# A quarter of w_o by a seven-product block scheme, woven with the rest of w_o by the list scheduler

## The chip, the cores and the metric

The kernel runs on one core of one Trainium2 chip. The metric is the device time of one execution in microseconds. The kernel before took 1211.24 us (median of three runs, 1210.77 to 1211.61); one more execution was taken with the profiler.

## The reference

One layer of a hybrid decoder trunk with 16 meta tokens and 256 tokens of width 2048, all in float32. The part that the change touches is the output projection of the mixer, `m @ W_o`, between the two gated branches and the first residual:

```python
u = rms_norm(h, g_pre_mix[l])
proj = u @ w_in[l]
...
m = jax.nn.sigmoid(gate_a) * y_a + jax.nn.sigmoid(gate_b) * y_b
h = h + rms_norm(m @ w_o[l], g_post_mix[l])
u = rms_norm(h, g_pre_mlp[l])
f = jnp.square(jax.nn.relu(u @ w_up[l])) @ w_down[l]
h = h + rms_norm(f, g_post_mlp[l])
```

`w_o` is 2048 x 2048, `w_up` 2048 x 8192, `w_down` 8192 x 2048. Only the 256 tokens go on after the mixer; they are two tiles of 128.

## The kernel before

**Arithmetic.** Every float32 product is made of three TensorE products: a value is split into a high part (float32r, a copy on ACT) and a low part (the difference, a subtraction on DVE), and high x high, high x low and low x high are summed in PSUM. So each weight chunk of 1 MB (four 128-row blocks by 512 columns) passes through ACT (`high`, line 253) and DVE (`low`, line 256) before TensorE can use it, and the activations are kept in both parts.

**Streaming.** `stream` (from line 188) lists all chunks up to the first columns of w_up. `open_chunk` (line 233) takes the next: it starts the load into one of three `raw` buffers on SP's queue, and appends the two splits. `fetch` (line 273) opens and splits two chunks ahead and hands out the oldest. The split parts lie in three buffers each (`part_tile`, line 226, number modulo 3). `spare` (line 204) gives up-chunks 1 and 2 rooms of their own in the tags s0 and s1.

**The mixer's end.** The conv-out projection (`project_t` with `evac_conv`, lines 814 to 830) makes the mixed features m in token order, 512 columns at a time; `to_features` (line 803) turns them with four TensorE transposes for each token tile and splits them into `m`.

**w_o.** Four column blocks `n` of 512, each four chunks `kc` deep. For the first three, `project_t` (line 693) runs, for each chunk, 12 matmuls for token tile 0 and 12 for tile 1 (`block_t`, line 683: the 128 x 128 block of m is stationary, 512 columns of the weight chunk stream past it). `evac_o` (line 884) takes the sum of squares (ACT) and multiplies by g (DVE). The last column block goes by `project_t_but_two` and `project_t_two` (lines 706 and 715): its last two chunks are run for tile 0 first and for tile 1 afterwards, so that tile 0's norm, residual and turn (lines 941 to 998) run under tile 1's products. Lines 931 to 935 open three up-chunks there and split them; the low part of the third follows at line 999.

**After it.** w_up and w_down are planned by `Plan` (line 22): each piece of work is added with its engine, a cost in us and the names that it reads and writes; `order` gives each a due time, which follows from TensorE's fixed order, and lists the pieces engine by engine as they could begin. w_down already goes by seven block products (steps P1 to P7 at line 1049) with sums of weight blocks on DVE (line 1120).

Lines that the prediction names: 688 (matmuls of `block_t`), 808, 810 and 811 (turn, copy, subtraction of m), 817 and 818 (evacuation of conv-out), 893 (residual), 910 (turn of h), 1132 and 1137 (splits inside the plan), 1286 (matmuls of w_down), 1308 (bank added to a block).

Of the kernel before, what the change touches and what calls it, by code (L numbers as in the profile page):

```python
# [100 lines left out]
def hybrid_block(ctx: ExitStack, tc: tile.TileContext, ins: dict, out: bass.AP):  # L101
# [39 lines left out]
    def misc_tile(name):  # L141
        return psB.tile([P, CW], F32, tag="misc", name=name)
# [66 lines left out]
    stream += columns(w_up, 0, KD, CW, HALF)  # L209
    FIRST = KD // HALF[0]  # L210
    opened = []
    at = {"n": 0}


    LINE = 16
    PLACES = {n: (2, 1) for n in standing_chunks}
    KEYS = [f"{tag}{b}" for tag in ("lo", "hi") for b in range(3)]
    ready = {}

# [3 lines left out]
    for key in KEYS:  # L223
        ready[key] = part_room(key, f"{key[:2]}_{key[2]}")

    def part_tile(tag, n):
        key = f"{tag}{n % 3}"
        room = ready.pop(key) if key in ready else part_room(key, f"{tag}_{n}")
        place = PLACES.get(n, (1, 1))[("hi", "lo").index(tag)]
        shift = (place - 1 - 3 * KEYS.index(key)) % 4 * LINE  # L230
        return room[:, shift:shift + CK * CW]

    def open_chunk(first=((2, nc.sync),) * 4):
        n = at["n"]
        at["n"] += 1
        src, (rows, width) = stream[n]
        raw = raws.tile([P, CK * CW], F32, tag="raw", name=f"raw_{n}")
        if n in spare:
            both = big.tile([P, 2, CK * CW], F32R, tag=spare[n], name=f"parts_{n}")
            hi, lo = both[:, 0, :], both[:, 1, :]  # L240
        else:
            hi, lo = part_tile("hi", n), part_tile("lo", n)
        raw, hi, lo = (t.rearrange("p (k c) -> p k c", k=rows) for t in (raw, hi, lo))
        pieces = rows if n < FIRST + 1 else 1
        k = rows // pieces
        i = 0
        for n_, queue in first if n < FIRST else ((rows, nc.sync),):
            sl = slice(i, i + n_)
            queue.dma_start(raw[:, sl, :], src[:, sl, :])
            i += n_  # L250

        def high(sl):
            nc.scalar.copy(hi[:, sl, :], raw[:, sl, :])  # L253

        def low(sl):
            nc.vector.tensor_sub(lo[:, sl, :], raw[:, sl, :], f32(hi[:, sl, :]))  # L256
# [7 lines left out]
        todo = [piece(i) for i in range(pieces)]  # L264
        if n in spare:
            todo = [lambda: high(slice(0, rows)), lambda: low(slice(0, rows))]
        opened.append((hi, lo, todo))

    def split_pieces(c):
        while opened[c][2]:  # L270
# [2 lines left out]
    def fetch(ahead=2):  # L273

        for c in range(ahead + 1):
            if c == len(opened) and at["n"] < len(stream):
                open_chunk()
            if c < len(opened):
                split_pieces(c)
        flush()  # L280
        return opened.pop(0)[:2]
# [421 lines left out]
            while after:  # L703
                after.pop(0)()

    def project_t_but_two(act, nk, accs):

        n = nk // CK
        for kc in range(n - 2):
            hi, lo = fetch()  # L710
            for t, acc in enumerate(accs):
                block_t(acc, hi, lo, act, kc, nk, t)
        return [fetch(1), fetch(0)]

    def project_t_two(act, nk, accs, two, t):

        for i, (hi, lo) in enumerate(two):
            block_t(accs[t], hi, lo, act, nk // CK - 2 + i, nk, t)


    sg = [None, None]

# [80 lines left out]
    def to_features(n, t, mt):  # L803

        def f():
            pt = misc_tile(f"mt_{n}_{t}").rearrange("p (k c) -> p k c", k=CK)
            for i in range(CK):
                nc.tensor.transpose(pt[:, i, :], mt[:, i * P:(i + 1) * P], ident)
            dst = m[:, n * CK:(n + 1) * CK, :, t * P:(t + 1) * P]
            nc.scalar.copy(dst[:, :, 0, :], pt)  # L810
            nc.vector.tensor_sub(dst[:, :, 1, :], pt, f32(dst[:, :, 0, :]))
        return f

    def evac_conv(n):
        def f(t, acc):
            mt = mts[:, (n * NT + t) % (CC // CW * 2), :]
            nc.vector.tensor_mul(mt, acc, sg[1][:, t, block(n)])
            nc.vector.tensor_add(mt, mt, sg[0][:, t, block(n)])
            blocks.append(to_features(n, t, mt))
        return f  # L820

    def s_act_of(k):
        return ln["out"][:, k, :, :]

    mts = big.tile([P, CC // CW * 2, CW], F32, tag="c", name="mts")
# [5 lines left out]
    after += blocks  # L831


    h1 = big.tile([P, NT, D], F32, tag="k8", bufs=2, name="h1")
    nc.gpsimd.dma_start(h1, xv)
    g_mix = big.tile([P, D], F32, tag="a", name="g_mix")
    nc.gpsimd.dma_start(g_mix, ins["g_post_mix"].broadcast_to([P, D]))
    og = big.tile([P, NT, D], F32, tag="k8", bufs=2, name="og")

    class Norm:  # L840

# [37 lines left out]
        nc.scalar.activation(junk, src, AF.Square, scale=scale, accum_out=norm[:, t, n:n + 1])  # L879

    def last_factor(dst, acc, n):
        nc.vector.tensor_mul(dst, acc, g_mix[:, block(n)])

    def evac_o(n):
        def f(t, acc):
            square_of(acc, norm1.ssq, t, n)
            last_factor(og[:, t, block(n)], acc, n)
            if n == NB - 2:
                norm1.start(t)
        return f  # L890

    def residual(t, n):
        nc.vector.scalar_tensor_tensor(
# [44 lines left out]
    def last_block(t):  # L938
        last_factor(og[:, t, block(NB - 1)], last_o[t], NB - 1)
# [10 lines left out]
        for i in range(CK):  # L950
            low(i)

    block_t(last_o[1], *two[0], m_of, NB - 2, KD, 1)
    block_t(last_o[1], *two[1], m_of, NB - 1, KD, 1, (0, 1))
    both(u2_tiles(0, 1, 0, CK))
    block_t(last_o[1], *two[1], m_of, NB - 1, KD, 1, (2, 3))
    square_of(last_o[1], norm1.ssq, 1, NB - 1)
    high, low = u2_tiles(0, 1, CK, CK)
    chain = norm1.steps(1)
# [8 lines left out]
    residual(1, 0)  # L968

    accs = acc_tiles("up00")  # L970
    ups = list(opened)
    opened.clear()

    def up_high(kc, t):

# [20 lines left out]
    last_block(1)  # L996
    residual(1, 3)
    residual(0, 3)
    ups[2][2].pop(0)()
    up_high(0, 1)  # L1000
    up_low(0)
    both(u2_tiles(1, 1, 2 * CK, CK))
# [101 lines left out]
            load(to_load.pop(0))  # L1104

    split_at = {}
    first_n = at["n"] - len(opened)
    for m_, (hi_, lo_, _) in enumerate(opened):
        split_at[m_] = {"hi": hi_, "lo": lo_}

    def weights(m_):

        while uses and uses[0][0] <= m_:
            done = len(last_use_order) - len(uses)
            _, what, raws_ = uses.pop(0)
            rooms = [room_at[r] for r in raws_]
            names = [f"raw{r}" for r in rooms]
            if what == "sum":
                a_, b_ = (room_of[r][:, :CK * CW] for r in rooms)
                plan.add("DVE", 2.29, lambda: nc.vector.tensor_add(a_, a_, b_),  # L1120
                         reads=names, writes=names[:1])
            else:
                box = split_at[m_] = {}
                raw = room_of[rooms[0]][:, :CK * CW]
                n, q = first_n + m_, (first_n + m_) % 3
                if products[m_][0][0] == "U":
                    PLACES[n] = (2, 1)
                rows, width = HALF if products[m_][0][0] == "U" else (CK, CW)

                def high():  # L1130
                    box["flat"] = part_tile("hi", n)
                    nc.scalar.copy(box["flat"], raw)  # L1132
                    box["hi"] = box["flat"].rearrange("p (k c) -> p k c", k=rows)

                def low():
                    lo = part_tile("lo", n)
                    nc.vector.tensor_sub(lo, raw, f32(box["flat"]))  # L1137
# [384 lines left out]
```

## Time and profile before

| | us |
|---|---|
| median of three runs | 1211.24 |
| profiled execution, its own time | 1211.07 |
| span of that execution, first to last instruction | 1209.1 |
| TensorE busy in the span | 1198.0 |
| VectorE (DVE) busy | 955.1 |
| ScalarE (ACT) busy | 615.9 |

The profile is of one execution on the core. PE rows are TensorE's matmuls, PEld its weight loads, POOL is GpSimd, and SPq and POOLq are the queues from which DMAs are issued. A row of a group gives the source line, the engine, the operation, output and input tiles, shape and count, then busy time, mean ns of one, and the idle time ahead of it with what ended it. A row of the timeline gives start, length, engine, line and operation; square brackets hold the idle time before it and its releaser. The conv-out projection runs from about 380 to 427 us, w_o from 427 to 515, and w_up and w_down from 515 on.

### The profile page before, as it was taken

What the parts mean: (1) busy time and instruction counts of PE and PEld (TensorE: products, weight loads), DVE (VectorE), ACT (ScalarE), POOL (GpSimd) and SP (SyncE); (2) the same over time, 40 slices, a digit from 0 to 9 for tenths busy, and PEclk for the clock granted to TensorE, in tenths of its full rate; (3) what the DMA queues carried; (4) which work ended last, traced back from release to release, by engine and by line L of the source; (5) the groups of instructions that cost most, each with busy time, mean ns of one, the idle gap of its engine ahead of it and who ended that gap; (6) DMA issues with size and microseconds to landing.
All of it is one profiled execution on the core that took longest, in us unless ns stands there. A gap on an engine that the chain in (4) does not pass through costs nothing.

```text
span 1209.1 us, 15692 instructions
## 1 busy us (share of the span) xinstructions
PE 1198.0 (99%) x6456; PEld 1040.1 (86%) x6456; DVE 955.1 (79%) x1039; ACT 615.9 (51%) x636; POOL 5.6 (0%) x17
## 2 busy tenths in 40 slices
PE   9999999999999999999999999999999999999996
PEld 9999988888888888898888888888888888888886
DVE  6799978999676654578988878878788778888756
ACT  7533344343584444465555564564554555555542
POOL 1000000000000000000000000000000000000000
PEclk9999999999999999999999999999999999999999
DMA  9655565556558655646475574674765764755841
GB/s 288 209 175 176 181 201 180 204 183 200 180 168 292 222 182 185 215 163 220 151 250 174 180 233 158 197 247 142 245 200 156 261 199 150 243 174 182 271 139 69
DMA packets 161510, 237.22 MB, mean 196 GB/s; under 512 B 4017, under 2 KB 91505, under 8 KB 160912
## 3 DMA queue, kind: packets, MB, share of 16 engines
q1 hardware_dynamic: 159648, 231.03, 58.4%
q0 software_dynamic: 624, 3.30, 0.7%
q10 hardware_dynamic: 1168, 1.91, 0.4%
q8 instruction: 50, 0.82, 0.3%
q14 instruction: 20, 0.16, 0.0%
HBM read 234.12 MB, written 2.10 MB: 195 GB/s over the span
## 4 chain that ended last, share of the span: by engine, by line
PE 99%; DVE 0%; DMA 0%; DVEq 0%; ACT 0%; issue 0%; ACTq 0%
PE bank_u L433 18%; PE acc_gate L688 14%; PE acc_up L1286 14%; PE bank_u L439 9%; PE bank_a L1286 7%; PE bank_b L1286 5%; PE acc_o L688 5%; PE acc_v L428 4%; PE acc_z L428 4%; PE acc_g L428 4%; PE acc_co L688 4%; PE acc_po L688 4%; PE acc_o_last L688 2%; PE acc_up L433 1%; PE bank_u L1286 1%; PE acc_up L439 1%
## 5 line engine op out<-in xcount | busy, mean ns | idle before, releaser
L433 PE MATMUL bank_u<-m,hi 128*128 128x512 f32 x960 | 329.9, 390 | 0.0
L253 ACT CAST hi<-raw 128x2048 fp32r<-128x2048 f32 (+1 forms) x114 | 180.5, 1596 | 226.5 <-PE acc_gate L688 71.5
L256 DVE TENSOR_TENSOR lo<-raw,hi 128x2048 fp32r<-128x2048 f32 (+1 forms) x114 | 215.0, 1895 | 74.6 <-ACT hi L253 74.2
L439 PE MATMUL bank_u<-m,lo 128*128 128x256 f32 x960 | 265.5, 277 | 0.0
L1137 DVE TENSOR_TENSOR lo<-raw_m,hi 128x2048 fp32r<-128x2048 f32 x85 | 194.4, 2289 | 58.3 <-ACT hi L1132 58.2
L1132 ACT CAST hi<-raw_m 128x2048 fp32r<-128x2048 f32 x85 | 162.5, 1912 | 137.9 <-PE bank_u L433 76.7
L433 PEld LDWEIGHTS bank_u<-m,hi 128*128 128x128 f32 x960 | 180.2, 188 | 37.9
L439 PEld LDWEIGHTS bank_u<-m,lo 128*128 128x128 f32 x960 | 180.3, 188 | 1.6
L688 PE MATMUL acc_gate<-hi,u 128*128 128x512 f32 x512 | 158.6, 390 | 0.0
L1286 PE MATMUL acc_up<-hi,forms 128*128 128x512 f32 x496 | 157.5, 389 | 0.0
L494 DVE SCALAR_TENSOR_TENSOR c<-a,taps,c 128x256 f32<-128x256 f32 x240 | 115.5, 484 | 7.1 <-ACT c L488 0.5
L688 PEld LDWEIGHTS acc_gate<-hi,u 128*128 128x128 f32 x512 | 96.1, 188 | 19.9
L1286 PEld LDWEIGHTS acc_up<-hi,forms 128*128 128x128 f32 x496 | 93.1, 188 | 19.5
L688 PE MATMUL acc_gate<-lo,u 128*128 128x512 f32 x256 | 99.6, 389 | 0.0
L1286 PE MATMUL acc_up<-lo,forms 128*128 128x512 f32 x248 | 96.6, 389 | 0.0
L1137 DVE TENSOR_TENSOR lo<-raw_c,hi 128x2048 fp32r<-128x2048 f32 x29 | 66.4, 2290 | 20.7 <-ACT hi L1132 20.7
L1286 PE MATMUL bank_a<-hi,forms 128*128 128x512 f32 (+1 forms) x256 | 82.0, 383 | 0.0
L1132 ACT CAST hi<-raw_c 128x2048 fp32r<-128x2048 f32 x29 | 55.3, 1908 | 50.7 <-PE bank_u L433 25.7
L1137 DVE TENSOR_TENSOR lo<-raw_a,hi 128x2048 fp32r<-128x2048 f32 x29 | 66.4, 2289 | 18.0 <-ACT hi L1132 18.0
L1132 ACT CAST hi<-raw_a 128x2048 fp32r<-128x2048 f32 x29 | 55.4, 1912 | 42.6 <-PE bank_u L433 19.4
L1286 PE MATMUL bank_b<-hi,forms 128*128 128x512 f32 (+1 forms) x200 | 63.7, 382 | 0.0
L688 PE MATMUL acc_o<-hi,m 128*128 128x512 f32 x192 | 59.6, 390 | 0.0
(275 smaller groups left out, 1766.4 us busy)
## 6 DMA issues: line engine op xcount, KB each, us to landing
raw<-in_w_in_dram SPq DMA_DIRECT2D x54, 1024.0 KB, 5.1
raw_m<-in_w_down_dram SPq DMA_DIRECT2D x37, 1024.0 KB, 5.4
raw_m<-in_w_up_dram SPq DMA_DIRECT2D x33, 1024.0 KB, 6.0
raw<-in_w_o_dram SPq DMA_DIRECT2D x16, 1024.0 KB, 5.2
raw_c<-in_w_down_dram SPq DMA_DIRECT2D x14, 1024.0 KB, 5.1
raw_a<-in_w_up_dram SPq DMA_DIRECT2D x13, 1024.0 KB, 5.8
raw_a<-in_w_down_dram SPq DMA_DIRECT2D x13, 1024.0 KB, 5.4
raw_c<-in_w_up_dram SPq DMA_DIRECT2D x12, 1024.0 KB, 5.7
```

What stands on the lines that cost most here:

```text
L253: nc.scalar.copy(hi[:, sl, :], raw[:, sl, :])
L256: nc.vector.tensor_sub(lo[:, sl, :], raw[:, sl, :], f32(hi[:, sl, :]))
L428: nc.tensor.matmul(acc, w[:, k[0], cs], act[:, k[1], a, off:], start=first and n == 0, stop=last and n == 2)
L433: nc.tensor.matmul(acc.rearrange("p (a t) -> p a t", a=2)[:, :, ts], hi[:, k[0], cs], act[:, k[1], :, off + ts.start:off + ts.stop], start ...
L439: nc.tensor.matmul(acc[:, :T], lo[:, k[0], cs], act[:, k[1], 0, off:], start=False, stop=stop, skip_group_check=True)
L494: nc.vector.scalar_tensor_tensor(c, conv["a"][:, q, i:i + T], taps[:, q, i:i + 1], c, op0=ALU.mult, op1=ALU.add)
L688: nc.tensor.matmul(acc, act(kk)[:, a_, ts_], w_[:, k, :], start=kk == 0 and n == 0, stop=kk == nk - 1 and n == 2)
L1132: nc.scalar.copy(box["flat"], raw)
L1137: nc.vector.tensor_sub(lo, raw, f32(box["flat"]))
L1286: nc.tensor.matmul(acc, forms[h][:, f, k, a_, :], box[w_][:, k, cs], start=start and k == 0 and n == 0, stop=stop and k == KH - 1 and n == ...
```

## The change

Write w_o's first two row blocks and first two column blocks as B11, B12, B21, B22 (each 512 x 512, the row block first) and m's tiles as A11, A12, A21, A22 (token tile first, then the 512-feature block). Instead of eight products A x B for this quarter, seven are formed, with sums of A's and of B's blocks (Winograd's form). `sums_of_m` forms the sums of A on DVE in place, from unsplit copies that `feature_steps` leaves in the tile `A`; `forms_o` splits them into `Sf`. The sums of B are formed in the raw rooms: B11 + B12 and B22 + B12 by a DMA from POOL's queue that adds what it loads to what lies there (`add_second`), the other two by DVE (`add_rooms`).

STEPS gives TensorE's order: `P1` to `P7` are the seven products (12 matmuls each), `Xnk` is column block n, row block k for both token tiles (24 matmuls), the last two of them for tile 0 alone. P2, P3 and P4 go straight into the banks of the result (`c00`, `c01`, `c10`); P1, P6, P7 sum up in bank `a` and P5 in `b`, from where ACT copies them to SBUF and DVE adds them to the result's banks. The raw chunks lie in five rooms: the three raw buffers and two in the tag s1 (free after the conv-out evacuation). The whole of w_o, the last turn of m, the evacuations of column blocks 0 to 2 and the loads and splits of the first three up-chunks are put into a `Plan` of their own. `stream` ends its w_o part after two chunks (row blocks 1 and 2 of column block 0), which are P2's and X02's.

```diff
@@ the stream
-    for n in range(NB):
-        stream += columns(w_o, 0, KD, n * CW)
-
-    spare = {len(stream) + 1: "s0", len(stream) + 2: "s1"}
+
+    stream += columns(w_o, CK, CK, 0) + columns(w_o, 2 * CK, CK, 0)
...
@@ the turn of m
+        def low():
+            nc.vector.tensor_sub(dst[:, :, 1, :], box["pt"], f32(dst[:, :, 0, :]))
+            if n < 2:
+                nc.scalar.copy(A[:, t, n], box["pt"])
...
+    def sums_of_m():
+
+        a11, a12, a21, a22 = (A[:, t, h] for t in range(2) for h in range(2))
+        nc.vector.tensor_sub(a11, a11, a21)
+        nc.vector.tensor_sub(a21, a21, a22)
+        nc.vector.scalar_tensor_tensor(a22, a11, -1.0, a22, op0=ALU.mult, op1=ALU.subtract)
+        nc.vector.tensor_add(a12, a12, a22)
...
@@ conv-out
-        after += blocks
+        after += blocks + [sums_of_m] * (n == 2)
...
@@ w_o
-    for n in range(NB - 1):
-        project_t(m_of, KD, evac_o(n), f"o{n}")
+    plan = Plan()
+    HALVES = ("hi", "lo")
+    SA1, SA2, SA3, SA4 = ((1, 0), (1, 1), (0, 0), (0, 1))
+    B_OF = {"P1": (0, 0), "P2": (1, 0), "P3": (1, 1), "P5": (0, 0), "P6": (0, 0), "P4": (0, 0),
+            "P7": (1, 1)}
+    A_OF = {"P1": (0, 0), "P2": (0, 1), "P4": (1, 1)}
+    FORM_OF = {"P3": SA4, "P5": SA1, "P6": SA2, "P7": SA3}
+    INTO = {"P1": "a", "P2": "c00", "P3": "c01", "P5": "b", "P6": "a", "P4": "c10", "P7": "a"}
+
+    GIVES_O = {"P1": [(0, 0, 1)], "P6": [(0, 1, -1)], "P7": [(1, 0, 1), (1, 1, -1)],
+               "P5": [(0, 1, 1), (1, 1, 1)]}
+    STEPS = "P2 X02 X20 P1 X12 P3 X21 P5 X22 P6 X03 P4 X23 P7 X13 X30 X31 X32 X33"
...
+    room_of = {b: opened[b][3] for b in range(2)}
+    room_of[2] = raws.tile([P, CK * CW], F32, tag="raw", name="raw_o2")
+    wide_room = big.tile([P, 2, CK * CW], F32, tag="s1", name="raw_o")
...
+    Sf = big.tile([P, NT, 2, CK, 2, P], F32R, tag="s0", name="forms_o")
+    free_rooms = [2, 3, 4]
...
+    def add_second(room):
+
+        src = source_o((0, 1))
+        plan.add("POOL", 1.0, lambda: nc.gpsimd.dma_start(room_view(room), src, accum_op=ALU.add),
+                 reads=(f"raw{room}",), writes=(f"raw{room}",), late=9.0)
...
+    def add_rooms(to, room):
+        a_, b_ = room_of[to][:, :CK * CW], room_of[room][:, :CK * CW]
+        plan.add("DVE", 2.29, lambda: nc.vector.tensor_add(a_, a_, b_),
+                 reads=(f"raw{to}", f"raw{room}"), writes=(f"raw{to}",))
+
+    def weights_o(i):
+        s = steps[i]
+        room = room_at[raw_key(s)]
+        if s == "P6":
+            add_rooms(room, room_at[B_OF["P3"]])
+            add_second(room_at[B_OF["P3"]])
+        if s == "P4":
+            add_rooms(room, room_at[B_OF["P2"]])
+        if i >= 2:
+            split_room(i, room)
+        if s == "P1":
+            add_second(room)
+        for key, last in last_use.items():
+            if last == i:
+                free_rooms.append(room_at[key])
+        loads_o()
...
+        if s in GIVES_O:
+            j = "ab".index(bank)
+            st = og[:, j, block(NB - 1)]
+            plan.add("ACT", 0.62, lambda: nc.scalar.copy(st, banks_o[bank]), reads=(bank,),
+                     writes=(f"st{j}",))
+            for t, n, sign in GIVES_O[s]:
+                def f(name=f"c{t}{n}", add_=(nc.vector.tensor_add if sign > 0 else
+                                             nc.vector.tensor_sub)):
+                    add_(banks_o[name], banks_o[name], st)
+                plan.add("DVE", 0.69, f, reads=(f"st{j}",), writes=(f"c{t}{n}",))
...
+    new_banks(acc_tile, "c00", "c10", "c01", "c11", "c02", "c12")
+    loads_o()
+    for f in (SA4, SA1, SA2, SA3):
+        forms_o(f)
+    plan.add("POOL", 1.0, load_g_mix, writes=("A", "g_mix"), late=3.0)
...
+    split_early(1, "s0", [f"S{t}{h}" for t in range(2) for h in range(2)])
+    late_low = split_early(2, "s1", ["raw3", "raw4"])
+    plan.emit()
...
@@ the last block
-    last_o = acc_tiles("o_last", NT)
-    two = project_t_but_two(m_of, KD, last_o)
-    while len(opened) < 3:
-        open_chunk()
-    split_pieces(1)
-    split_pieces(0)
-    opened[2][2].pop(0)()
-    project_t_two(m_of, KD, last_o, two, 0)
```

`split_room` adds the ACT copy and the DVE subtraction of a room's block to the plan, as lines 1130 to 1140 do; `loads_o` adds a load on SP as soon as a room is free, and up-chunks only into rooms 0 to 2; `multiply` runs the 12 matmuls of a product. The load of `g_mix` moves from line 837 into the plan, behind the splits of the forms, since it takes the room of `A`.

More of the change, by code (lines that the diff above doesn't have):

```diff
@@ L263, in piece @@
             return f
[L264 to L267, printed above, removed]
+        opened.append((hi, lo, [piece(i) for i in range(pieces)], flat))
     def split_pieces(c):
@@ new lines, in load_g_mix, with evac_o @@
+    def load_g_mix():
+        later["g_mix"] = g = big.tile([P, D], F32, tag="a", name="g_mix")
+        nc.gpsimd.dma_start(g, ins["g_post_mix"].broadcast_to([P, D]))
+    def evac_o(n, t, bank):
+        plan.add("ACT", 0.92, lambda: square_of(banks_o[bank], norm1.ssq, t, n), reads=(bank,),
+                 writes=("junk", f"ssq{t}"))
+        plan.add("DVE", 0.69, lambda: last_factor(og[:, t, block(n)], banks_o[bank], n),
+                 reads=(bank, "g_mix"), writes=(f"og{t}{n}",))
+    new_banks(acc_tile, "c00", "c10", "c01", "c11", "c02", "c12")
@@ new lines, in hybrid_block @@
+    loads_o()
+    for f in (SA4, SA1, SA2, SA3):
+        forms_o(f)
+    plan.add("POOL", 1.0, load_g_mix, writes=("A", "g_mix"), late=3.0)
+    for i in range(2):
+        weights_o(i)
+    for i, s in enumerate(steps):
+        for w in range(max(i, 2), min(i + 3, len(steps))):
+            if w not in boxes:
+                weights_o(w)
+        if s == "P1":
+            new_banks(misc_tile, "a", "b")
+        if s == "X30":
+            for t in range(NT):
+                plan.add("PE", 0.0, lambda t=t: banks_o.update({f"c{t}3": acc_tile(f"o_c{t}3")}),
+                         writes=(f"c{t}3", f"c{t}0"))
+        product_o(i)
+        if i == 0:
+            for t in range(NT):
+                m_last(t)
+        done = {"P7": (0,), "X23": (2,), "X13": (1,)}.get(s, ())
+        for n in done:
+            for t in range(NT):
+                evac_o(n, t, f"c{t}{n}")
+        if s == "X13":
+            for t in range(NT):
+                plan.add("DVE", 0.4, lambda t=t: norm1.start(t), reads=(f"ssq{t}",),
+                         writes=(f"v{t}",))
@@ new lines, in hybrid_block, with split_early, high, low @@
+    split_room(len(steps), room_at["U", 0], CK, True)
+    at["parts"] = first_p + len(steps) + 1
+    at["n"] += 3
+    early = {}
+    def split_early(n, tag, gone):
+        raw = room_of[room_at["U", n]][:, :CK * CW]
+        def high():
+            early[n] = both = big.tile([P, 2, CK * CW], F32R, tag=tag, name=f"parts_up{n}")
+            nc.scalar.copy(both[:, 0, :], raw)
+        def low():
+            nc.vector.tensor_sub(early[n][:, 1, :], raw, f32(early[n][:, 0, :]))
+        name = f"raw{room_at['U', n]}"
+        plan.add("ACT", 1.91, high, reads=(name,), writes=[f"early{n}"] + gone)
+        if n == 2:
+            return low
+        plan.add("DVE", 2.29, low, reads=(name, f"early{n}"), writes=(f"early{n}",))
@@ L998, in hybrid_block @@
     residual(0, 3)
-    ups[2][2].pop(0)()
+    late_low()
     up_high(0, 1)
```

191 lines of the change are left out of this document (139 added, 52 removed).

## The prediction, made before the change ran

> **What bounds the kernel now.** I read the page's busy times and chain first, then what TensorE waited for, then single stages.
>
> ```profile
> span 1209.1 us, 15692 instructions
> PE 1198.0 (99%) x6456; PEld 1040.1 (86%) x6456; DVE 955.1 (79%) x1039; ACT 615.9 (51%) x636; POOL 5.6 (0%) x17
> PE 99%; DVE 0%; DMA 0%; DVEq 0%; ACT 0%; issue 0%; ACTq 0%
> ...
> PE idle L349 <- POOL ident masks.py:199: 1.4, 1, 1.4
> PE xm L361 <- DMA m_in<-in_meta_dram: 0.5, 1, 0.5
> ```
>
> TensorE sets the end: 99% of the chain is its own work, and its only two waits lie in the first microseconds. Time leaves only where matmuls leave. The duration in a row (0.39 us) is not the price of a matmul, since neighbours overlap; the price is the distance between starts.
>
> ```profile
> L688 PE MATMUL acc_po<-hi,y x128: 389/389/396, 336.9 to 380.2; 128*128 128x512 f32 x128
> L688 PE MATMUL acc_po<-lo,y x64: 389/389/397, 337.1 to 380.0; 128*128 128x512 f32 x64
> ...
> 567.67 0.39 PE L1286 MATMUL acc_up<-lo,forms 128*128 128x512 f32 x1
> ...
> 570.39 0.39 PE L1286 MATMUL acc_up<-lo,forms 128*128 128x512 f32 x1
> ```
>
> 128 + 64 matmuls start between 336.9 and 380.2: 43.3 / 191 = 0.2267 us each. The second stretch is the w_down stage, whose stationary operand also comes from tags s0 and s1: 12 matmuls in 2.72 us, the same. Twelve of them are one block product (128 tokens by one 512x512 block of weights).
>
> **The change, part by part.** *Removed from TensorE:* w_o is 16 chunks, each for two token tiles, so 32 block products. After, STEPS has 7 P steps of one product and 12 X steps of two: 31. Gain 12 x 0.2267 = **2.72 us**. The turns of the mixed features are as many as before.
>
> *Added to DVE and ACT around it.*
>
> ```profile
> 426.50:513.20 86.70, 86.70 (x388) 71.87 (x387) 46.27 (x39) 37.97 (x34) 0.00 (x0) 1.00 0.61 198
> 541.20:1190.00 648.80, 648.80 (x3336) 554.87 (x3335) 521.55 (x453) 353.96 (x333) 0.00 (x0) 1.00 0.60 196
> ...
> L1137 DVE TENSOR_TENSOR lo<-raw_m,hi 128x2048 fp32r<-128x2048 f32 x85 | 194.4, 2289 | 58.3 <-ACT hi L1132 58.2
> L1132 ACT CAST hi<-raw_m 128x2048 fp32r<-128x2048 f32 x85 | 162.5, 1912 | 137.9 <-PE bank_u L433 76.7
> L1308 DVE TENSOR_TENSOR F_raw<-F_raw,bank_a 128x512 f32<-128x512 f32 x25 | 17.0, 680 | 0.0
> L811 DVE TENSOR_TENSOR m<-mt,m 128x512 fp32r<-128x512 f32 x8 | 5.2, 686 | 9.0 <-ACT m L810 9.0
> L810 ACT CAST m<-mt 128x512 fp32r<-128x512 f32 x8 | 4.3, 591 | 15.9 <-PE mt L808 15.9
> ```
>
> Columns of the first two rows: stretch, its length, then busy us of PE, weight load, DVE, ACT, POOL. In the w_o stage DVE gets three more splits (19 products for 16 chunks: 3 x 2.29), two sums of weight blocks (the split's shape, 2 x 2.29), four low parts of the forms and six additions into banks (10 x 0.69, the bank rows' 0.68 rounded up): 18.4 us. 46.3 + 18.4 = 64.7 of 84.0 us, 77%. ACT gets 3 x 1.91 + 8 copies x 0.59 = 10.5: 48.5 us, 58%. The second row is w_up and w_down, built by the same planner with sums, bank additions and splits: DVE 80%, and TensorE still filled the whole stretch. So throughput is covered; what can cost is a late piece.
>
> *Steady order.* Split i starts when product i-3 frees its buffer and must be done when product i starts; P and X alternate, so 2.72 + 5.44 = 8.16 us lie between.
>
> ```profile
> 426.69 0.39 PE L688 MATMUL acc_o<-hi,m 128*128 128x512 f32 x1
> 426.89 1.92 ACT L253 CAST hi<-raw 128x2048 fp32r<-128x2048 f32 x1 [3.01 <-PE acc_co L688]
> 427.45 0.69 DVE L817 TENSOR_TENSOR mts<-acc_co,sg 128x512 f32<-128x512 f32 x1
> 428.17 0.69 DVE L818 TENSOR_TENSOR mts<-mts,sg 128x512 f32<-128x512 f32 x1
> ...
> 431.90 0.40 PE L688 MATMUL acc_o<-hi,m 128*128 128x512 f32 x1
> 432.93 0.48 PE L688 MATMUL acc_o<-hi,m 128*128 128x512 f32 x1
> ```
>
> ACT begins 0.20 us after the last matmul's slot ends (426.89 against 426.69), so a split takes 0.20 + 1.91 + 0.03 + 2.29 = 4.4 of the 8.16; the slack of 3.7 holds one weight sum (2.29) or two bank additions (1.4). I take zero; if sum and additions meet in one gap the excess is near 0.
>
> Now count from 426.69, the start of P2. Turning the last features, now behind P2 alone, needs mts at 428.86, that is 2.17, against P2's end at 2.72: no wait. The turns take 1.03 - 0.23 = 0.80. Products then end at X02 8.96, X20 14.40, P1 17.12, X12 22.56, P3 25.28, X21 30.72, P5 33.44, X22 38.88, P6 41.60, X03 47.04, P4 49.76, X23 55.20, P7 57.92, X13 63.36.
>
> *Before the plan:* four sums of m (4 x 0.69 on DVE, in co2) and four copies to A (ACT, 0.59). Before L811 alone DVE stood idle 9.0 us over the four column blocks, and a split there has two chunks, 10.9 us, for its 4.4: zero. If that cover were gone, the 2.8 us of the sums would be the loss.
>
> *The adding DMAs.* They load w_o's block 01 onto a room from POOL's queue; before has none.
>
> ```profile
> raw<-in_w_o_dram SPq DMA_DIRECT2D x16, 1024.0 KB, 5.2
> h<-in_x_dram POOLq DMA_DIRECT2D x1, 2048.0 KB, 11.2
> g_mix<-in_g_post_mix_dram POOLq DMA_DIRECT2D x1, 1024.0 KB, 13.7
> ```
>
> Block 00 goes to a room of s1, free when sg1 is last read at 428.14 (1.45); landing 6.65, split done 10.9, adding DMA issued. Its reader is P5's split, which must start by 30.72 - 4.3 = 26.4: **15.5 us** of cover. The second is issued behind the first weight sum (P5's split 22.8 to 27.0, sum to 29.3) and must land by P7's split at 50.9: 21.6 us. Ends for one DMA: 5.2 (plain) and 13.7 (POOL's slowest, issued right behind the 2 MB of h); both are covered, so zero. An adding DMA also reads its destination; were it twice the 13.7, it would not be covered (rival 3). The load of g_mix moves behind the forms on the same queue, one landing (13.7) before the evacuation of column block 0 near 47 needs it.
>
> [...] No row here shows a POOL DMA issued under a split. [...]
>
> *P7 into X13.* P7's result goes through a copy (ACT) into two banks (DVE), and X13's second token tile writes one of them, 2.72 us after P7. X30's split is then at work: hi 55.40 to 57.31, lo to 59.63. Copy 58.12 to 58.71; bank addition 59.63 to 60.32 against 60.64. Just fits; if the other bank is served first, 0.4 lost. I take **0.1**.
>
> *The turn into w_up.* The chain after the last tile-0 product and the split of up chunk 2 stay; their margin is small already.
>
> ```profile
> 508.46 1.91 ACT L253 CAST parts<-raw 128x2048 fp32r<-128x2048 f32 x1 [1.38 <-DMA raw<-in_w_up_dram]
> 512.25 1.42 DVE L893 SCALAR_TENSOR_TENSOR h<-og,r_mix,h 128x512 f32<-128x512 f32 x2
> 513.28 0.60 PE L910 MATMUL ht<-ident,h 128*128 128x128 f32 x4
> ```
>
> The turn at 513.28 needs the first residual, done near 512.97: 0.3 us. Chunk 2 still comes in behind the split of the last w_o block, so nothing moves; zero.
>
> What does move are the three buffers of raw: they follow rooms 0, 1, 2, which hold up chunks 1, 2, 0. So chunk 4, not chunk 5 as before, now loads behind the late low part of chunk 2.
>
> ```profile
> 530.29 0.37 SPq L249 DMA_DIRECT2D raw<-in_w_up_dram  x1
> 536.46 1.91 ACT L253 CAST hi<-raw 128x2048 fp32r<-128x2048 f32 x1 [1.58 <-DMA raw<-in_w_up_dram]
> 538.40 2.29 DVE L256 TENSOR_TENSOR lo<-raw,hi 128x2048 fp32r<-128x2048 f32 x1 [1.17 <-ACT hi L253]
> 541.17 0.40 PE L433 MATMUL bank_u<-m,hi 128*128 128x512 f32 x1
> 541.40 0.28 PE L439 MATMUL bank_u<-m,lo 128*128 128x256 f32 x1
> ...
> DMA to landing us min/median/max: 5.1/5.5/8.0
> ```
>
> These rows are chunk 5's; with chunk 4 in its place lo ends at 540.69, needed at 541.40 by the first product of the plan. It fits by 0.7 with this landing (530.29 to about 536.4); with the slowest landing of the group, 8.0, it loses 1.2. I take 0. Behind it ACT's queue (squares of h1, copies of banks) and DVE's slide by about 2 us.
>
> Sum: -2.72 + 0.1 = -2.62. The profiled run took 1211.07 (span 1209.1 and 1.97 around it), 0.17 under the median 1211.24; with the median, **1208.6**.
>
> **The rivals.** 1: *the whole saving* (under 0.3 lost), 1208.5 to 1208.8. For it: TensorE's dense second row above. 2: *the joints eat it*: P7 into X13 (0.4), chunk 4 (1.2), one split behind a sum (1) each lose a little: 1209.0 to 1211.2, by all three 1211.1. For it: margins of 0.3 and 0.7; against it, every such margin in the rows holds. 3: *the adding DMAs are late*, the other side. Place: P5's split, which waits at the head of ACT's queue with X22's split behind it. Price: landing less 15.5; twice 13.7 gives 27.4 - 15.5 = 11.9 at P5 and 27.4 - 21.6 = 5.8 at P7, so 1226. It decides the sign beyond 15.5 + 2.6 + 2.4 = 20.5 us. 4: *another late piece*: an in-order queue with a split that waits for a load (5.2) ahead of urgent bank work, two or three times: 1214 to 1222. The planner's fixed costs allow it; the w_down stage speaks against it. 5: *no saving*: the form tiles give a longer distance between matmuls. 48 matmuls (P3, P5, P6, P7) would each need 0.05 more; the forms row at 0.2267 speaks against it: 1211.
>
> **How the numbers follow.** Chances: rival 1, the forecast, 0.55; 2, 0.27; 3, 0.10; 4, 0.06; 5, 0.02. A measurement of this kernel can tell about 0.2%, 2.4 us, from no change; the whole saving is only just above that. Faster 0.55 (1), same 0.29 (2 and 5), slower 0.16 (3 and 4). Range: low 1208.0 (the fastest run shown, 1210.77, less 2.72), high 1212.0, through 1, 2 and 5, with most of 3 and 4 outside; by the first case alone 1208.0 to 1209.0.
>
> **What would show it.** Right: 12 fewer matmuls, no wait of TensorE between 426 and 1190, products 2.72 us long, the turn of h at about 510.5. Rival 2: small TensorE waits at X13's second tile or at the first bank_u matmul. Rival 3: ACT's hi before P5 waiting for a DMA from POOL longer than 15.5 us. Rival 4: TensorE waiting on a split behind another DMA. Wrong altogether: a distance other than 0.2267 in the P products, or a loss outside the stage.

## The result, and the profile after

The changed kernel takes 1208.1 us (median of 11 runs, 1207.76 to 1209.21) against 1211.4 us of the kernel before on the same chip (11 runs, 1210.77 to 1211.87): ratio 0.9976, 95% interval 0.9966 to 0.9985. The forecast was 1208.6 us. The saving of 2.72 us would be a ratio of 0.9978, inside that interval. The profiled execution took 1208.15 us.

The page of the changed kernel: the span, the busy times, one DMA queue and all that TensorE waited for.

```profile
span 1206.4 us, 15712 instructions
PE 1195.8 (99%) x6444; PEld 1038.4 (86%) x6444; DVE 974.7 (81%) x1058; ACT 627.6 (52%) x651; POOL 8.3 (1%) x19
...
q0 software_dynamic: 1680, 5.40, 1.7%
...
PE idle L343 <- POOL ident masks.py:199: 1.4, 1, 1.4
PE xm L355 <- DMA m_in<-in_meta_dram: 0.5, 1, 0.5
```

6456 matmuls became 6444, the span went from 1209.1 to 1206.4, and TensorE still waits only in the first microseconds. The two adding DMAs show as two more GpSimd instructions and, on its queue, as 5.40 MB moved (3.30 before; the two loads are 2.1).

Where the time left is seen between two instructions that both kernels have: the last matmul of conv-out and the first turn of h. This is the TensorE timeline of the changed kernel, cut to the ends of P2 and P7 and that turn (start, length, instruction):

```profile
426.75 0.39 PE L682 MATMUL acc_co<-hi,s_act 128*128 128x512 f32 x1
426.98 0.39 PE L1020 MATMUL o_c<-hi,m 128*128 128x512 f32 x1
...
429.70 1.03 PE L790 MATMUL mt<-ident,mts 128*128 128x128 f32 x8
...
482.30 0.39 PE L1020 MATMUL o_a<-hi,forms_o 128*128 128x512 f32 x1
...
485.02 0.39 PE L1020 MATMUL o_c<-hi,m 128*128 128x512 f32 x1
...
510.87 0.66 PE L1151 MATMUL ht<-ident,h 128*128 128x128 f32 x4
```

From 426.75 to 510.87 are 84.1 us; before, from 426.46 (one slot ahead of the 426.69 that the prediction counts from) to 513.28, 86.8: 2.7 less, all of it here. P2 runs 426.98 to 429.70 and P7, whose stationary operand is a form of m's sums, 482.30 to 485.02: both 2.72. The turn of m stands right behind P2.

The stage as a window (stretch, length, then busy us of PE, weight load, DVE, ACT and POOL, granted clock, DMA share, GB/s):

```profile
426.98:511.02 84.04, 84.04 (x376) 69.48 (x375) 63.03 (x54) 47.86 (x45) 3.17 (x3) 1.00 0.78 249
```

DVE went from 46.3 to 63.0 us (75%), ACT to 47.9, and TensorE is busy from end to end at full clock.

### The profile page after: what moved, and what is told of

It is laid out like the page before. It is cut to its first block, busy times and chain, and to the rows that moved or that the text cites. A ratio compares the mean times of both kernels' runs of the same rounds, so it can differ in the third digit from the quotient of the medians.

```text
span 1206.4 us, 15712 instructions
## 1 busy us (share of the span) xinstructions
PE 1195.8 (99%) x6444; PEld 1038.4 (86%) x6444; DVE 974.7 (81%) x1058; ACT 627.6 (52%) x651; POOL 8.3 (1%) x19
## 3 DMA queue, kind: packets, MB, share of 16 engines
q10 hardware_dynamic: 1168, 1.91, 0.4%
## 4 chain that ended last, share of the span: by engine, by line
PE 99%; DVE 0%; DMA 0%; DVEq 0%; ACT 0%; issue 0%; ACTq 0%
PE bank_u L427 18%; PE acc_gate L682 14%; PE acc_up L1516 14%; PE bank_u L433 9%; PE bank_a L1516 7%; PE o_c L1020 6%; PE bank_b L1516 5%; PE acc_v L422 4%; PE acc_z L422 4%; PE acc_g L422 4%; PE acc_co L682 4%; PE acc_po L682 4%; PE acc_up L427 1%; PE bank_u L1516 1%; PE o_a L1020 1%; PE acc_up L433 1%
## 5 line engine op out<-in xcount | busy, mean ns | idle before, releaser
L250 ACT CAST hi<-raw 128x2048 fp32r<-128x2048 f32 (+1 forms) x99 | 151.7, 1548 | 188.9 <-PE acc_gate L682 71.5
L253 DVE TENSOR_TENSOR lo<-raw,hi 128x2048 fp32r<-128x2048 f32 (+1 forms) x99 | 180.6, 1835 | 44.1 <-ACT hi L250 43.8
L1020 PE MATMUL o_c<-hi,m 128*128 128x512 f32 x208 | 65.6, 390 | 0.0
```

Of the source, the lines that this page charges most:

```text
L1020: nc.tensor.matmul(acc, form(k, a_), box[w_][:, k, :], start=start and k == 0 and n == 0, stop=stop and k == CK - 1 and n == 2, skip_group ...
```

## The experiments

All ratios are against the kernel before, run on the same chip in the same rounds. A second run of the changed kernel stood beside the first three experiments: 1208.09 us, ratio 0.9975 (0.9965 to 0.9984). Beside the others stood only the kernel before, at 1211.3 to 1211.5 us; where they are set against the changed kernel, 1208.1 is meant.

### The same plan with eight products

```diff
-STEPS = "P2 X02 X20 P1 X12 P3 X21 P5 X22 P6 X03 P4 X23 P7 X13 X30 X31 X32 X33"
+STEPS = "X01 X02 X20 X00 X12 X11 X21 X10 X22 X03 X23 X13 X30 X31 X32 X33"
...
-        after += blocks + [sums_of_m] * (n == 2)
+        after += blocks
...
-    for f in (SA4, SA1, SA2, SA3):
-        forms_o(f)
```

The rooms and the planning of the whole of w_o stay; all that the seven products need is gone, the copies to A too, and column block 0 is taken out after X03.

> All of w_o in the list scheduler's plan, with the five rooms and the early up-chunks, but the quarter by eight plain products (16 X steps, no P steps; the sums of m and of w_o, the forms and the adding DMAs are left out, the result is the same). Theory M: TensorE has its 32 block products again, so the time is that of the kernel before, ratio 0.9995 to 1.0005, and TensorE has no wait in the stage. Rival W: part of the saving stays, ratio 0.998 to 0.999.

Measured 1210.99 us, ratio 0.9998 (0.9989 to 1.0007). Its window over the stage:

```profile
426.50:513.50 87.00, 86.95 (x388) 71.78 (x387) 45.97 (x39) 37.92 (x34) 0.00 (x0) 1.00 0.63 217
```

With the 12 matmuls back (388 records in the stage for 376), 87.05 us lie between the last matmul of conv-out (426.46) and the first turn of h (513.51), where before had 86.8, and the time is that of before. The new order of loads and splits is worth nothing by itself that the interval of 0.1% would show: the gain is the 12 matmuls.

### P7's two additions served in the other order

```diff
+            if s == "P7":
+                def both_banks():
+                    nc.vector.tensor_add(banks_o["c10"], banks_o["c10"], st)
+                    nc.vector.tensor_sub(banks_o["c11"], banks_o["c11"], st)
+                plan.add("DVE", 1.38, both_banks, reads=(f"st{j}",), writes=("c10", "c11"))
+                return
```

> P7's result is added to bank c10 first and to c11 after it, in one piece of the plan; everything else as in the changed kernel. In the profile after, the first of the two additions ended at 487.3 and the second at 487.9, and X13's second tile, which needs c11, began at 487.74. Theory C (that bank addition is the tightest joint of the stage, margin 0.3 to 0.4 us): TensorE now waits 0.2 to 0.5 us before X13's second tile, and the time rises by as much. Rival: something else holds that tile, no gap, time unchanged within 0.1.

Measured 1208.43 us, ratio 0.9974 (0.9965 to 0.9983), not to be told from the changed kernel by its time. The timelines tell it. First DVE and TensorE of the changed kernel around X13's second token tile:

```profile
484.44 2.29 DVE L981 TENSOR_TENSOR lo<-raw,hi 128x2048 fp32r<-128x2048 f32 x1 [1.25 <-ACT hi L976]
486.65 1.29 DVE L1059 TENSOR_TENSOR o_c<-o_c,og 128x512 f32<-128x512 f32 x2
...
487.51 0.62 PE L1020 MATMUL o_c<-hi,m 128*128 128x512 f32 x2
```

Then those of the experiment:

```profile
487.18 0.69 DVE L1058 TENSOR_TENSOR o_c<-o_c,og 128x512 f32<-128x512 f32 x1
487.78 0.69 DVE L1059 TENSOR_TENSOR o_c<-o_c,og 128x512 f32<-128x512 f32 x1
...
488.04 0.99 PE L1020 MATMUL o_c<-hi,m 128*128 128x512 f32 x2
```

The row of two TensorE matmuls holds the last of tile 0 and the first of tile 1. Tile 1 needs the bank c11. The row is 0.62 long in the changed kernel, where c11 was served first, and 0.99 in the experiment, where it came second (its `L1059`): 0.37 of waiting inside a row, too short for the page's list of waits. That is the 0.4 which the prediction gave for this order, and it reaches the end of the stage: from the last matmul of conv-out (427.28) to the first turn of h (511.79) are 84.5 us here, 84.1 in the changed kernel. The reader sees too that both additions stand behind the split's low part on DVE, in both kernels.

### Without the adding DMAs

```diff
     def add_second(room):
+        return
```

> The two adding DMAs are left out (P5 and P7 then use B11 and B22 alone, so a quarter of w_o's product is another one); everything else stays. Theory H (the adding DMAs are wholly hidden): time within 0.1% of the changed kernel, ratio to before 0.9973 to 0.9983. What they cost elsewhere should show in the loads beside them: the slowest load of the stage took 12.0 us from issue to landing beside the first one; without it 5 to 7. Rival: they cost time through the loads that they slow; then 0.5 us or more faster than the changed kernel.

Measured 1208.07 us, ratio 0.9971 (0.9960 to 0.9981); no wait of TensorE in the stage. What the DMAs do to their neighbours shows in the list of DMA issues (issuing queue, count, KB each, median us to landing), first of the changed kernel, then without them:

```profile
raw_o<-in_w_o_dram SPq DMA_DIRECT2D x10, 1024.0 KB, 7.5
...
raw_o<-in_w_o_dram POOLq DMA_DIRECT2D x1, 1024.0 KB, 11.0
g_mix<-in_g_post_mix_dram POOLq DMA_DIRECT2D x1, 1024.0 KB, 13.3
raw<-in_w_o_dram POOLq DMA_DIRECT2D x1, 1024.0 KB, 9.7
```

```profile
raw_o<-in_w_o_dram SPq DMA_DIRECT2D x10, 1024.0 KB, 5.9
...
g_mix<-in_g_post_mix_dram POOLq DMA_DIRECT2D x1, 1024.0 KB, 6.0
```

The two adding DMAs of 1 MB landed after 11.0 and 9.7 us. With the two of them the ten loads of the first row have a median of 7.5 us instead of 5.9; the one issued at 441.0, behind the first of them, landed after 12.0 us and without it after 6.9, the one at 458.6, behind the second, after 10.8 and 5.0. The load of g_mix right behind the first on its queue takes 13.3 instead of 6.0. All of that lies under TensorE's work.

### The adding DMAs twice, one behind the other

```diff
-        plan.add("POOL", 1.0, lambda: nc.gpsimd.dma_start(room_view(room), src, accum_op=ALU.add),
-                 reads=(f"raw{room}",), writes=(f"raw{room}",), late=9.0)
+        for _ in range(2):
+            plan.add("POOL", 1.0, lambda: nc.gpsimd.dma_start(room_view(room), src, accum_op=ALU.add),
+                     reads=(f"raw{room}",), writes=(f"raw{room}",), late=9.0)
```

> Each adding DMA is issued twice, one after the other on POOL's queue (B12 is added twice, so a quarter of w_o's product is another one). In the profile after, the first was issued at 438.5 and landed 11.0 us later, at 449.5; P5's split can start at 449.8 and must start by 457.7 - 4.4 = 453.3. Theory K (cover of 15 us, as the prediction had it): the second landing falls at 459 to 460, so P5 begins 6 to 7 us late and the time rises by 5.5 to 8 us over the changed kernel (ratio to before 1.002 to 1.005); the pair behind the first weight sum fits its 21 us nearly, under 1 us more. Rival: more cover than thought (the split is not at the head of the queue, or the second addition is faster), rise under 3 us.

Measured 1219.49 us, ratio 1.0069 (1.0054 to 1.0084): 11.4 us over the changed kernel, more than expected. Its timeline (the first adding DMA, TensorE around its waits, the first turn of h), and a window behind the first waits (the clock is the third number from the end):

```profile
438.25 1.32 POOL L960 DMA_DIRECT2D raw_o<-in_w_o_dram  x1 [56.63 <-DVE lo L982]
...
457.25 0.39 PE L1021 MATMUL o_c<-hi,m 128*128 128x512 f32 x1
462.30 0.79 PE L1021 MATMUL o_b<-hi,forms_o 128*128 128x512 f32 x1 [4.67 <-ACT hi L977]
464.62 0.79 PE L1021 MATMUL o_b<-lo,forms_o 128*128 128x512 f32 x1 [1.53 <-DVE lo L982]
...
469.91 0.42 PE L1021 MATMUL o_c<-lo,m 128*128 128x512 f32 x1
...
484.58 0.50 PE L1021 MATMUL o_c<-lo,m 128*128 128x512 f32 x1 [0.86 <-DVE lo L982]
...
493.95 0.50 PE L1021 MATMUL o_a<-lo,forms_o 128*128 128x512 f32 x1 [0.87 <-DVE lo L982]
...
522.62 0.66 PE L1152 MATMUL ht<-ident,h 128*128 128x128 f32 x4
```

```profile
464.00:468.00 4.00, 3.38 (x8) 2.70 (x9) 2.86 (x2) 0.99 (x1) 0.56 (x1) 0.50 0.00 0
```

P5 (bank o_b) waits for its high part and then for its low part: two distances of 5.05 and 2.32 us where 0.2267 is the usual one, 6.9 lost. The high part's split takes 1.91 and 0.03 lie behind it, so the second addition had landed by 460.4; with the first issued at 438.25 that is 22.1 us for two, which less the 15.5 of cover makes 6.6. The two later waits, in P4 (484.58) and P7 (493.95), cost about 1.2 each, distances counted. They are no late landing: the list of this kernel has X23's split ahead of P4's and X13's ahead of P7's on ACT, other than the changed kernel's, and the second pair of additions landed 21.3 us after its first issue. The rest is the clock. Behind the first waits TensorE was granted half of it (0.50), and the twelve distances from 464.62 to 469.91 took 5.29 us in place of 2.72, 2.6 lost. 6.9 + 2.6 + 2.4 = 11.9; from the last matmul of conv-out (426.43) to the first turn of h are 96.2 us in place of 84.1, 12.1 more. The 0.50 stands behind the 4.7 us wait, but the mean clock from 456 to 464, 0.73, puts its fall at about 459.7 (an estimate; its window is in the last section), when TensorE had stood still for 2.0 us.

### The low parts of the P blocks twice

```diff
-            nc.vector.tensor_sub(lo, raw, f32(box["flat"]))
+            for _ in range(times):
+                nc.vector.tensor_sub(lo, raw, f32(box["flat"]))
+        times = 2 if i < len(steps) and steps[i][0] == "P" else 1
...
-        plan.add("DVE", 2.29, low, reads=(f"raw{room}", f"hi{q}"), writes=(f"lo{q}",))
+        plan.add("DVE", 2.29 * times, low, reads=(f"raw{room}", f"hi{q}"), writes=(f"lo{q}",))
```

> DVE subtracts the low part of each of the seven P blocks twice (same values, result unchanged): 7 x 2.29 = 16 us more of DVE in the stage, from 63.0 of 84.0 us (75%) to 79 (94%). Theory D (DVE has room in the mean, but not in each gap of 8.16 us between a split's start and its use): a gap with two splits, one doubled, a weight sum and a bank addition needs 4 x 2.29 + 0.7 = 9.9, so P6 and P4 come about 2 us late each, and the time rises by 2 to 6 us. Rival (mean throughput alone counts): 94% fits, rise under 0.5.

Six blocks were doubled, not seven, since P2's split lies outside the plan: 13.7 us more on DVE. Measured 1211.92 us, ratio 1.0005 (0.9995 to 1.0014): 3.8 us lost. A window over its stage and one inside it, then two rows of its TensorE timeline that end in a wait, and a third wait from its list:

```profile
428.00:513.00 85.00, 82.91 (x369) 68.01 (x367) 73.58 (x55) 46.58 (x45) 3.17 (x3) 1.00 0.76 243
```

```profile
460.00:466.00 6.00, 4.51 (x20) 3.40 (x19) 5.96 (x3) 4.06 (x3) 1.28 (x1) 1.00 0.64 105
```

```profile
462.02 0.50 PE L1022 MATMUL o_c<-lo,m 128*128 128x512 f32 x1 [1.49 <-DVE lo L982]
...
471.07 0.50 PE L1022 MATMUL o_c<-lo,m 128*128 128x512 f32 x1 [0.60 <-DVE lo L982]
```

```profile
PE ht L1153 <- DVE h L885: 0.7, 1, 0.7
```

DVE is at 73.6 of 85 us (87%) over the stage, still short of full, but between 460 and 466 it is busy for 5.96 of 6.0 us, and there the products are late. The stage's own average is not the limit; the stretch with a doubled split, a sum of weights and the next split in a row is. The waiting products are not P6 and P4, as I had expected, but the X products just before them, whose low parts stand behind the doubled ones. The third wait is a consequence further on: at the first turn of h, tile 0's square stands on ACT behind the split of up-chunk 2, which waited for its load until 509.44 (506.27 in the changed kernel). The clock stays at 1.00 behind the wait of 1.5 us.

### The P products back to back

```diff
-STEPS = "P2 X02 X20 P1 X12 P3 X21 P5 X22 P6 X03 P4 X23 P7 X13 X30 X31 X32 X33"
+STEPS = "P2 X02 X20 X12 X21 X22 P1 P3 P5 P6 P4 P7 X03 X23 X13 X30 X31 X32 X33"
```

> The same 19 steps in another order: the P steps P1 P3 P5 P6 P4 P7 one behind the other instead of between X steps. Theory V (the alternation is the cover): P5 waits for the adding DMA issued behind P1's split, which has now two products less than in the weave, and each P gives a split only 5.4 us for its 4.4 with the weight sums (2.29) and bank additions (0.7 each) on top; loss 10 to 25 us, the kernel slower than before (ratio 1.006 to 1.02). Rival (the planner finds room in any order): loss under 3 us.

Measured 1220.95 us, ratio 1.0083 (1.0068 to 1.0098). In this kernel column block 0 was still taken out after P7, ahead of X03, so X03's share is missing from what it gives out. It was run again with that block taken out after X03:

```diff
-        done = {"P7": (0,), "X23": (2,), "X13": (1,)}.get(s, ())
+        done = {"X03": (0,), "X23": (2,), "X13": (1,)}.get(s, ())
```

> The changed kernel with its P steps back to back (P1 P3 P5 P6 P4 P7 behind the X steps that come before, X03 X23 X13 behind them), so a split has 3 x 2.72 = 8.16 us only where X steps lie between, and 2.72 us each in the run of P steps, for 2.29 us of split, and sums, copies and bank additions on top. Column block 0 is taken out after X03, so all of w_o's result is computed. Theory W (the weaving matters: without it the pieces are late, TensorE waits on splits in the run of P steps, and its clock falls behind waits above some 4 us as it did with the doubled adding DMAs): over 1213 us, waits of TensorE on lo or hi between 460 and 490, 1215 to 1221 us in all. Theory B (the list scheduler's order covers it, buffers run ahead during the X steps): within 1 us of the changed kernel's 1208.1, no wait in the stage over 1 us.

Measured 1220.95 us again, ratio 1.0079 (1.0063 to 1.0094): 12.9 us over the changed kernel. The rows of its TensorE timeline that end in a wait, then DVE over the time of the first three, then two windows:

```profile
466.00 0.50 PE L1020 MATMUL o_b<-lo,forms_o 128*128 128x512 f32 x1 [1.83 <-DVE lo L981]
...
470.31 0.50 PE L1020 MATMUL o_a<-hi,forms_o 128*128 128x512 f32 x1 [1.50 <-ACT hi L976]
472.64 0.80 PE L1020 MATMUL o_a<-lo,forms_o 128*128 128x512 f32 x1 [1.82 <-DVE lo L981]
...
479.28 0.80 PE L1020 MATMUL o_c<-lo,m 128*128 128x512 f32 x1 [1.82 <-DVE lo L981]
```

```profile
463.65 2.29 DVE L981 TENSOR_TENSOR lo<-raw_o,hi 128x2048 fp32r<-128x2048 f32 x1 [1.10 <-ACT hi L976]
465.98 2.29 DVE L988 TENSOR_TENSOR raw_o<-raw_o,raw_o 128x2048 f32<-128x2048 f32 x1
470.29 2.29 DVE L981 TENSOR_TENSOR lo<-raw_o,hi 128x2048 fp32r<-128x2048 f32 x1 [2.02 <-ACT hi L976]
```

```profile
468.00:472.00 4.00, 1.31 (x5) 0.52 (x3) 1.98 (x2) 2.39 (x2) 1.29 (x1) 1.00 0.28 32
472.00:476.00 4.00, 3.36 (x8) 2.69 (x9) 3.97 (x4) 1.00 (x1) 0.00 (x0) 0.57 1.09 201
```

P5's low part, the sum of weights in the same room, P6's high part and P6's low part follow one another, 463.65 to 472.58: 6.6 us from low part to low part, where a product lasts 2.72. Woven, X products of 5.44 us lie between and cover that chain. The first wait lies ahead of it: P5's split began at 461.71 behind the copy of P1's bank on ACT, near the landing of the adding DMA (issued at 452.16, median 9.0 us), and the trace doesn't part the two. The clock falls here too, to a mean of 0.57 from 472 to 476, though no wait is longer than 1.83 us: of the four microseconds before, TensorE had worked 1.31. The "some 4 us" of theory W was the author's reading of one wait, the 4.67 us of the doubled DMAs; here the clock fell with shorter ones.

### A buffer of the tag raw given away ahead of up-chunk 4

```diff
     open_chunk()
+    gap = raws.tile([P, CK * CW], F32, tag="raw", name="raw_gap")
+    nc.gpsimd.memset(gap[:, 0:16], 0.0)
```

This was to price the one step of the prediction that had failed in place (below). Its trace shows that it does not.

> The changed kernel with one buffer of the tag raw given away behind chunk 5's turn, so that the chunk before it loads where the prediction put it: behind the late low part of w_up's chunk 2 (near 525.7 + 2.3 = 528.0 us) instead of near 505.8. A write of 16 columns on GpSimd is all that is added. The step of the prediction that failed in place was this one; here its price is measured alone. As the prediction has it (theory M): chunk 4 issued near 528, landed near 534, its high part done near 536, its low part near 538.3 us, the first product of the plan near 538.9 takes it with 0.7 us to spare: no wait, 1208.1 to 1208.5 us. Rival L (the landing is the slow one of the group, or the split is queued behind squares and copies): a wait of TensorE of 0.5 to 1.5 us at the first products of w_up, 1208.8 to 1209.8 us. Rival S (the split behind it slides, and several low parts of w_up are late in turn): waits past 545 us too, over 1210 us.

Measured 1207.74 us, ratio 0.9969 (0.9957 to 0.9980), no wait in the stage. Its timeline on GpSimd, SP and ACT:

```profile
506.01 0.11 POOL L1238 MEMSET raw_gap<- 128x16 f32 x1 [47.59 <-DVE lo L981]
500.97 5.55 SPq L246 DMA_DIRECT2D raw<-in_w_up_dram  x2
528.13 0.37 SPq L246 DMA_DIRECT2D raw<-in_w_up_dram  x1
530.76 1.92 ACT L250 CAST hi<-raw 128x2048 fp32r<-128x2048 f32 x1
534.32 1.91 ACT L250 CAST hi<-raw 128x2048 fp32r<-128x2048 f32 x1 [1.64 <-DMA raw<-in_w_up_dram]
```

The kernel opens and splits chunks 3, 4 and 5 in this order. The SP row of two holds the loads of chunks 3 and 4, the second of them issued at 506.15, right behind the write to the buffer given away (506.01 + 0.11): chunk 4 got that same buffer back, at nearly the time of the changed kernel (505.80). The load at 528.13 is chunk 5's, as before; its split waits for it at 534.32, behind chunk 4's at 530.76. So chunk 4 was not moved, the time is that of the changed kernel, and neither theory M nor its rivals were tested.

## Why the prediction was right, point by point

**The gain.** Right: 12 fewer matmuls, 2.7 us from the stage and nothing elsewhere. The eight-product kernel shows it is theirs. The distance in the products on forms was 2.72 / 12 too, so rival 5 (a longer distance) falls.

**DVE and ACT.** Predicted 64.7 and 48.5 us in the stage, measured 63.0 and 47.9. That throughput was covered held, with one limit that I had not seen: the doubled low parts cost 3.8 us at 87%, so the average said less than the local chain. The window of 8.16 us for a split of 4.4 was the right quantity; the back-to-back order, which takes it down to two P products, 5.44, lost 12.9.

**The turn of m, the sums of m.** The turn waits for nothing at 429.70, as predicted from a readiness of 2.17 against P2's 2.72. The sums cost nothing.

**The adding DMAs.** Bounds of 5.2 and 13.7 us, measured 11.0 and 9.7. P5's split, ready to run at 449.86, waits for another thing, its buffer:

```profile
438.48 1.32 POOL L959 DMA_DIRECT2D raw_o<-in_w_o_dram  x1 [56.58 <-DVE lo L981]
...
449.86 1.91 ACT L976 CAST hi<-raw_o 128x2048 fp32r<-128x2048 f32 x1 [3.04 <-PE o_c L1020]
```

Landed at 438.48 + 11.0 = 449.5, it was 4.5 us inside the 15.5 of cover. Doubled, it was late by what that cover leaves. Two things in rival 3 were mis-sized. The landing of twice 13.7 was too long: two in a row took 22.1. And its price was the landing less the cover, which gives 6.6 at P5 and nothing at P7 (21.3 against 21.6). The run lost 6.9 at P5, 2.6 more to the clock behind it, and 2.4 where the list had put other splits first. So the sign would have turned at an earlier landing than the 20.5 that I gave. The prediction had no row of a DMA issued on POOL under a split; here the first issue took 1.32 us (from 438.48) with a split on DVE beside it (438.69 to 440.98), and the second 1.28 (from 456.96; split 456.33 to 458.62).

**P7 into X13.** I took 0.1 between 0 and 0.4. The kernel has 0 (the bank that X13 needs is served first); the other order shows the 0.4 as 0.37 in the trace.

**The turn of h.** Predicted about 510.5, measured 510.87, with no wait; 510.5 had left out that conv-out ended 0.3 later in this execution.

**The step that failed: up-chunk 4.** "They follow rooms 0, 1, 2 ... So chunk 4, not chunk 5 as before, now loads behind the late low part of chunk 2" is wrong. The SP queue of the changed kernel, its load behind the late low part being the last:

```profile
505.80 0.37 SPq L246 DMA_DIRECT2D raw<-in_w_up_dram  x1
...
528.01 0.37 SPq L246 DMA_DIRECT2D raw<-in_w_up_dram  x1
```

Chunk 4 was loaded at 505.80, and chunk 5 alone at 528.01, as before. Chunk 4 took the buffer that came free first, not the next one by room number; in the last experiment too it took the one free at 506.12, ahead of the one that chunk 2's late low part held. The kernel before had said so, in rows that I had and did not set side by side: its low parts on DVE, then the loads on SP.

```profile
505.30 2.29 DVE L256 TENSOR_TENSOR parts<-raw,parts 128x2048 fp32r<-128x2048 f32 x1 [2.56 <-ACT parts L253]
507.51 2.28 DVE L256 TENSOR_TENSOR lo<-raw,hi 128x2048 fp32r<-128x2048 f32 x1
```

```profile
507.62 2.57 SPq L249 DMA_DIRECT2D raw<-in_w_up_dram  x2
```

Each load follows the end of a low part, whichever came first (505.30 + 2.29 = 507.59, then 507.51 + 2.28 = 509.79). That the step cost nothing, as the sum has it, is luck, since no chunk 4 was loaded there. What the step would have cost is not measured. Chunk 5 ends its low part at 536.04 + 2.29 = 538.33, and the first low part of the plan, chunk 4's, is used at 539.12; in its place chunk 4 would have had 0.8 us to spare, near the 0.7 of the prediction. That is argued, and the 1.2 us that rival 2 put on it were not tested either.

**The sum.** −2.62 predicted, −2.7 in the trace; the profiled executions stand 2.92 apart and the medians 3.3, with 2.7 inside the interval. Some 0.15 us of the 3.3 lie outside the span: a run's time less its span is 1.94 us in the mean for the kernel before and 1.79 for the changed one (1.77 with eight products, so it is not the matmuls'). The rest of what the medians show beyond 2.7 is not settled.

## What to carry to other kernels

In this stage, where TensorE was busy from end to end, a matmul taken away was worth its distance (12 x 0.2267 us, 2.7 measured), and the rest of the work is to show that every piece that feeds it still has a window: count the serial chain between two products (load, high part, low part, sum) against the products that lie between, since the busy share of the whole stage can hide a local jam (87% with the doubled low parts, 5.96 of 6.0 us inside). The cover of a transfer as a number told here what a late landing costs: 22.1 us against 15.5 gave 6.6, and 6.9 were lost. Price a wait that might come by its length and by the clock behind it (6.9 and 2.6 us with the doubled DMAs), and look at waits that lie close together as a group (1.83, 1.50 and 1.82 us in the back-to-back run, with a mean clock of 0.57 behind them).

## What the runs showed of the hardware that was not expected

The clock halved not only at one wait of 4.7 us (0.50 from 464 to 468, doubled DMAs) but also at a row of waits of 1.5 to 1.8 us with little work between (0.57 from 472 to 476, back-to-back order); a lone wait of 1.5 us left it at 1.00 (460 to 466, doubled low parts). In these traces the length of a wait does not decide it: in the back-to-back run the wait of 1.83 us that ended at 466.00 has 1.00 behind it, the one of 1.82 us that ended at 479.28 has 0.50. Windows of the back-to-back run, then of the doubled DMAs (the clock is the third number from the end):

```profile
466.00:468.00 2.00, 2.00 (x9) 1.65 (x10) 2.00 (x1) 0.00 (x0) 0.00 (x0) 1.00 0.00 0
...
472.00:474.00 2.00, 1.36 (x3) 1.16 (x4) 1.97 (x2) 0.00 (x0) 0.00 (x0) 0.61 1.06 194
474.00:476.00 2.00, 2.00 (x6) 1.53 (x5) 2.00 (x3) 1.00 (x1) 0.00 (x0) 0.54 1.13 208
476.00:478.00 2.00, 1.40 (x5) 0.58 (x4) 1.18 (x2) 1.93 (x2) 0.00 (x0) 1.00 1.06 297
478.00:480.00 2.00, 0.72 (x2) 0.63 (x3) 2.00 (x2) 2.00 (x2) 0.00 (x0) 0.82 0.75 288
480.00:482.00 2.00, 2.00 (x6) 1.55 (x5) 2.00 (x2) 1.16 (x2) 0.00 (x0) 0.50 0.71 207
482.00:484.00 2.00, 2.00 (x8) 1.50 (x7) 2.00 (x2) 0.32 (x1) 0.00 (x0) 0.83 0.84 325
```

```profile
456.00:464.00 8.00, 2.42 (x9) 1.30 (x7) 2.64 (x2) 1.90 (x1) 0.00 (x0) 0.73 0.81 216
464.00:468.00 4.00, 3.38 (x8) 2.70 (x9) 2.86 (x2) 0.99 (x1) 0.56 (x1) 0.50 0.00 0
468.00:472.00 4.00, 4.00 (x14) 3.14 (x14) 2.58 (x2) 3.14 (x3) 0.73 (x1) 0.76 0.66 92
```

With 1.00 and 0.50, the values of whole windows, as the only two, these means put the changes of the clock at about 472.4, 475.9, 479.3 and 482.7 in the back-to-back run and at 459.7 and 469.9 with the doubled DMAs: an estimate, 3.4 us from one to the next in the first run and 10.2 in the second. In the 3.4 us ahead of the three falls TensorE had worked 0.50, 1.55 and 1.35 us (469.03 to 472.44 and 475.85 to 479.26; 456.28 to 459.69), but also only 1.57 in the 3.4 us ahead of 466.00, and there the clock stayed at 1.00. What lets it fall is not shown by these runs.

The adding DMAs slowed their neighbours: the plain loads of w_o took 7.5 us in the median instead of 5.9, and the 1 MB load issued on GpSimd's queue 0.85 us behind the first of them landed after 13.3 us instead of 6.0. How much of the last is the adding is open: in the kernel before, the same load right behind a plain one of 2 MB took 13.7.
